# A two-block transformer kernel: one convolution tile instead of two on the vector engine, and the final sum by column halves

## The chip, the cores and the metric

The kernel runs on one core of one Trainium2 chip (trn2). The metric is the device time of one execution in microseconds (us). Engines: PE (TensorE, matrix products; PEld is its weight load), DVE (VectorE), ACT (ScalarE), POOL (GpSimd), SP (SyncE, which here only issues transfers).

## What is computed

Everything is float32, for 256 tokens of width 1024. A first block (two layers of mixer, feed-forward and gated side input) runs first and isn't touched. A second block follows, cut here to what matters:

```
h = rmsnorm(x, norm_mix_g) * (1 + sc1) + sh1
u = h @ w_in + b_in;  a, gt = split(u, 2);  u = a * sigmoid(gt)          # [256, 1024]
y = depthwise causal convolution of u, 31 taps per channel, + b_dw
y = silu(layernorm(y, ln_g, ln_b)) @ w_out
x = x + g1 * y
h = rmsnorm(x, norm_ffn_g) * (1 + sc2) + sh2
x = x + g2 * moe(h)      # 32 experts in 4 groups, top 2 in one group, hidden width 512
return rmsnorm(x, final_g)
```

## The kernel before, in words

**Order of work.** The program fixes the order on each engine by hand; every engine takes its instructions in program order. Three helpers place work between the matrix products of a stage: `fill` (lines 101 to 104) runs a function after so many products, `background` (lines 114 and 115) gives one small piece of work after every 12th or, from line 1418 on, every 10th product, and `prep` (lines 155 to 177) loads the next weight block (1 MB, SP) and splits an earlier one into a high and a low float32r part (ACT copies the high part, DVE subtracts; tiles `hl`). A float32 product is made of three products of such parts (`mm3`, `passes`).

**Convolution stage.** The 1024 channels are eight tiles of 128, with channels on partitions and 256 tokens along the row. For tiles 0 to 2 the input product is made token-major and turned (lines 1287 to 1306, `turn_u`); for tiles 3 to 7 it is made channel-major (`conv_in_proj`, step `i3` to `i7`, 48 products each). `conv_u` (line 1176) makes the gate with ACT and DVE. The tiles below `ONDVE` (line 1860: 2, so tiles 0 and 1) are convolved on DVE: `conv_dve` (line 1244) puts 31 taps per tile, each a `scalar_tensor_tensor` of 128x256, into `background`. The other tiles are convolved on PE: `u` goes to DRAM (`ud`, issued by POOL, line 1194) and comes back four-fold shifted (`u4`, four transfers issued by SP, line 1199; step `r`), POOL builds the diagonal tap blocks (`conv_taps_w`, line 1170; three buffers), and `conv_pe` (line 1257, steps `c2` to `c7`) makes 32 products, takes up to 8 pieces of background, and then lets ACT or DVE read the result into `yc`. The steps run in the order of `TG["plan"]` (line 1887): `R` and `t` prepare the router, `s` (`conv_pivot`, line 1271) computes the mean of two tiles (`PIVOT`, line 1889), which is subtracted from all, and `p` calls `prep`.

**Layer norm.** `conv_sums` (line 1210) squares each tile on ACT and adds tile and square into running sums: on DVE for tiles 0 and 1 and for the last two (`LATE`, tiles 6 and 7), on POOL for the others. After the last tile PE reduces the sums over the partitions (line 1458), DVE and POOL make mean and inverse deviation, PE spreads them (`mb`, `rb`), and per tile DVE subtracts and scales, ACT applies silu and makes the high part, DVE the low part (lines 1484 to 1494). `warm(n)` (line 123) issues n products whose result nobody reads. Then comes the product with `w_out`, the router and the experts.

**Experts.** Sixteen pairs of experts run one after the other; a pair takes twelve weight blocks of 1 MB in six steps of two (gate 0 and 1, up 2 and 3, down 4 and 5). `preload` (line 1120) issues block q into slot q % 21 as soon as the 21 slots allow; all are SP's. `down` (line 1636) turns the hidden values, multiplies by the two down blocks, and makes a high and a low part `yh`, `yl` that `combine2` of the next pair adds into the four PSUM banks `acc`. For the last pair `way_back` (line 1599) gives a plain float32 matrix, and `down` multiplies the result by a row of gains (`scaled`).

**The end.** Before the last pair's down product `gather_up` moves `acc` to SBUF and adds x; `acc` is zeroed by products with `zo` (line 1773). Then a loop of n_more rounds (line 1787; it runs for experts with more than 64 tokens) follows, and after it `finish`: eight float32 products into `acc` (`combine`, line 1671, four of 512 columns), DVE adds, ACT squares with a row sum, POOL the power, `spread(1)` (line 1713: the final gain row over all partitions, PE and then a copy), four DVE products, and four output transfers from SP.

Of the kernel before, what the change touches and what calls it, by code (L numbers as in the profile page):

```python
# [18 lines left out]
D = 1024  # L19
# [21 lines left out]
def kernel(ctx, tc, A, out, stop=None):  # L41
# [1119 lines left out]
    squares = cp.tile([128, 4, 256], F32, name="squares", tag="row")  # L1161
# [8 lines left out]
    def conv_taps_w(m):  # L1170

        taps[m] = cu.tile([128, 32, 32], F32, name="taps", tag="taps", bufs=3)
# [3 lines left out]
    def conv_u(m, pt):  # L1176
        sg = cu.tile([128, 256], F32, name="sg", tag="sg", bufs=2)
        act(sg, pt[:, 256:512], AF.Tanh, scale=0.5, bias=hbias[:, 8 + m:9 + m])
        a_ = cu.tile([128, 256], F32, name="a_", tag="a_", bufs=2)
        act(a_, pt[:, 0:256], AF.Identity, scale=0.5, bias=hbias[:, m:m + 1])  # L1180
# [6 lines left out]
        stt(u[:, 30:286], sg, 1.0, a_, ADD, MUL)  # L1187
# [8 lines left out]
        def back(q=SP):  # L1196
            u4[m] = cu.tile([128, 4, 284], F32, name="u4", tag="u4", bufs=3)
            for j in range(4):
                q.dma_start(u4[m][32 * j:32 * j + 32],
# [7 lines left out]
    sums = {"pool": None, "dve": None}  # L1207
    kept, squared = [], []

    def conv_sums(m):  # L1210

        sq = squares[:, len(squared) % 2, :]
# [3 lines left out]
        if m < ONDVE:  # L1216
            kept.append(new)
            if len(kept) == 2:
                sums["dve"] = small.tile([128, 2, 256], F32, name="sums", tag="xf")
                for i in range(2):  # L1220
                    tt(sums["dve"][:, i, :], kept[0][i], kept[1][i], ADD)
        elif m in LATE:
            for i in range(2):
                if m == LATE[0]:
                    tt(sums["dve"][:, i, :], sums["dve"][:, i, :], sums["pool"][:, i, :], ADD)
                tt(sums["dve"][:, i, :], sums["dve"][:, i, :], new[i], ADD)
        elif sums["pool"] is None:
            sums["pool"] = squares[:, 2:4, :]
            for i in range(2):
                G.tensor_copy(sums["pool"][:, i, :], new[i])  # L1230
        else:
            for i in range(2):
                tt(sums["pool"][:, i, :], sums["pool"][:, i, :], new[i], ADD, e=G)
# [49 lines left out]

    first_w = [nxt(True) for _ in range(3)]
    pm = [psum("mm") for _ in range(3)]
    um, us = {}, {}
    for h in range(2):
# [4 lines left out]
        for m in range(3):  # L1292
# [4 lines left out]
            um[m, h] = cu.tile([128, 256], F32, name="um", tag="um", bufs=4)  # L1297
# [121 lines left out]
    for m in range(ONDVE, ONDVE + 3):  # L1419
        conv_taps_w(m)  # L1420
    for step in TG["plan"].split():
# [3 lines left out]
        elif step in "ra":  # L1425
            while reads:
                reads.pop(0)(SP if step == "r" else S)
        elif step == "o":
            preload(len(moe_w) + 1)
        elif step[0] == "c":  # L1430
            conv_pe(m)
            if m < 5:
                conv_taps_w(m + 3)
# [17 lines left out]
    cs_ = [psum("aux"), psum("aux")]  # L1451
    mb, rb = psum("tp"), psum("tp")
# [3 lines left out]
    for i in range(2):  # L1456
        for h in range(2):
            T.matmul(cs_[i][:, h:h + 1], sums["dve"][:, i, h * 128:(h + 1) * 128], per_d, start=True, stop=True)
        if i == 0:
            V.tensor_copy(mo_[:, 0:2], cs_[0][:, 0:2])  # L1460
            tt(mo_[:, 2:4], mo_[:, 0:2], mo_[:, 0:2], MUL)
# [3 lines left out]
    stt(lv[:, 0:2], cs_[1][:, 0:2], EPS, mo_[:, 2:4], ADD, SUB)  # L1465
# [133 lines left out]
    def way_back(oh_g, n, exact=False, into=None):  # L1599
# [4 lines left out]
        if exact:  # L1604
# [5 lines left out]
        og_ = into or moe.tile([128, 2, 128], F32, name="ogT", tag="ogT", bufs=1)  # L1610
        V.tensor_copy(og_[:n], tp[:n, 0:256].rearrange("p (h t) -> p h t", h=2))  # L1611
        return og_
# [23 lines left out]
    def down(hid, weights, n_e, y, before=lambda j: None, scaled=False, gates_of=None):  # L1636
# [8 lines left out]
        py = [pbank("w"), pbank("w")]  # L1645
        for b in range(4, 6):
            ws = weights(b)
            before(b)
            for kk in range(2):
                k = 2 * (b - 4) + kk  # L1650
                for c in range(2):
                    for e in range(n_e):
                        T.matmul(py[c][64 * e:64 * e + 64, :], hT[:, k, 64 * e:64 * e + 64],  # L1653
                                 ws[e][:, kk * 1024 + c * 512:kk * 1024 + (c + 1) * 512],
                                 start=k == 0, stop=k == 3)
        if scaled:
            for c in range(2):
                sl = slice(512 * c, 512 * c + 512)
                tt(y[:n, sl], py[c][:n], end[0][:n, sl], MUL)
        else:  # L1660
            gc = gates_of()
            for c in range(2):
                sl = slice(512 * c, 512 * c + 512)
                act(yh[:, sl], py[c], AF.Copy, scale=gc)
                stt(yl[:, sl], py[c], gc, yh[:, sl].bitcast(F32), MUL, SUB)
# [40 lines left out]
    def start_ends():  # L1706
# [4 lines left out]
        end.extend([rows_[:, 0:D], rows_[:, D:2 * D], R, ring.tile([128, 2048], F32, name="raw", tag="raw")[:, 0:D]])  # L1711
# [39 lines left out]

    for i in range(NP):
        def weights(b, i=i):
# [3 lines left out]

        final = i == NP - 1

        def back(j, i=i, prev=prev, final=final):  # L1760
# [6 lines left out]
            if j == 1:  # L1767
                backs[i] = way_back(onehots[i], 128, not final)
            if i == NP - 2 and j == 5:
                start_ends()  # L1770
            if final and j == 5:
                for a in acc.values():
                    T.matmul(a, zo[:, 0:1].to_broadcast([1, 128]), zo[:, 1:2].to_broadcast([1, 512]), start=True, stop=False)
# [4 lines left out]
        hid = expert(weights, 2, (lambda: spread(0)) if final else None, None if i else start, 128 * (i % 2))  # L1778
        down(hid, weights, 2, end[3] if final else None, back, scaled=final, gates_of=lambda i=i: backs[i][1])
        prev = backs[i]  # L1780


    bt = rtile("bt", 1, pool=moe)
    V.memset(bt, 0.0)
    spare = nexts.tile([128, 2048], F32, name="nw", tag="nw")
    n_more = nc.values_load(nblk[0:1, 0:1], min_val=0, max_val=7)
    with tc.For_i(0, n_more, 1):
        oe = spare[:, D + 256:D + 288]
        ts(oe, upto, bt, None, ALU.is_gt)
        stt(oe, before, bt, oe, ALU.is_le, MUL)  # L1790
        tmp = moe.tile([128, 32], F32, name="more", tag="more")
        sel = moe.tile([128, 8], F32, name="sel")

        def pick(j, src):
            tt(tmp, src, oe, MUL)
            red(sel[:, j:j + 1], tmp, ADD)
        for h in range(2):
            pick(h, rank[:, h, :])
            pick(2 + h, gate[:, h, :])
        pick(4, before)  # L1800
        pick(5, iota64[:, 0:32])
        tt(sel[:, 6:7], bt, sel[:, 4:5], SUB)
        ts(sel[:, 6:7], sel[:, 6:7], 1.0, 64.0, ADD, MUL)
        ts(sel[0:1, 5:6], sel[0:1, 5:6], FAR, None, ADD)
        eid = moe.tile([1, 1], I32, name="eid")
        V.tensor_copy(eid, sel[0:1, 5:6])
        e_reg = nc.values_load(eid[0:1, 0:1], engines=(mybir.EngineType.SP,), min_val=0, max_val=NEXP - 1)
        oh_r = spare[:, D + 288:D + 544].rearrange("p (h t) -> p h t", h=2)
        oh_g = moe.tile([128, 2, 128], F32, name="oh", tag="oh_g", bufs=1)
        for h in range(2):  # L1810
            tt(sel[:, h:h + 1], sel[:, h:h + 1], sel[:, 6:7], SUB)
            for t_, sc in ((oh_r, rstd[h][:, 0:1]), (oh_g, sel[:, 2 + h:3 + h])):
                ts(t_[:, h, 0:64], iota64, sel[:, h:h + 1], sc, EQ, MUL)
        gather(oh_r, 64)
        og_ = way_back(oh_g, 64, into=spare[:, D:D + 256].rearrange("p (h t) -> p h t", h=2))

        def weights(b):
            t_ = wring.tile([128, 2048], F32, name="wr", tag="wr")
            SP.dma_start(t_, A["moe"][bass.ds(e_reg, 1), b].rearrange("a p n -> p (a n)"))
            return [t_]  # L1820
        hid = expert(weights, 1)
        y2 = spare[:, 0:D]
        down(hid, weights, 1, y2, scaled=True)
        for h in range(2):
            combine(h, og_, y2, False, False, 64)
        ts(bt, bt, 1.0, None, ADD)
    last = {}
    R, frow = end[2], end[1]

    def finish(h):  # L1830
        for c in range(2):
            sl = slice(512 * c, 512 * c + 512)
# [192 lines left out]
```

## Time and profile before

| what | us |
|---|---|
| median of three runs | 1257.26 (1253.07 to 1257.48) |
| the profiled execution, its own time | 1258.29 |
| its span in the profile | 1256.5 |
| PE, busy | 1191.1 (95%) |
| DVE, busy | 655.1 (52%) |
| ACT, busy | 481.4 (38%) |
| POOL, busy | 76.0 (6%) |

The profile counts microseconds from the start of the span. A row of the timeline gives start, duration, engine, line of the kernel, operation, output and inputs, and how many like instructions were merged; in square brackets stands how long the engine had been idle before and what ended that. The first block ends at about 659 us, the convolution stage runs to about 750, its output product and the router to about 796, the experts to about 1230, and the end to 1256.5. Durations of matrix products are pipelined, so two of them overlap in a row; one float32 product is two records.

### The profile page before, as it was taken

The numbers are of one execution on the slowest core, as the hardware profiler recorded it, in microseconds if no ns is written. First come the engines' busy times: TensorE is split into PE (matmuls) and PEld (weight loads), VectorE is DVE, ScalarE is ACT, GpSimd is POOL, SyncE is SP. The second block draws the span as 40 slices with busy tenths as digits, with TensorE's granted clock in tenths as the row PEclk, the third lists the DMA queues.
The fourth block names the chain that finished last, engine by engine and source line by source line (L and its number), as shares of the span: only waits on it lengthen the run. The fifth ranks groups of instructions, "written<-read, shape, count | busy, mean of one in ns | idle before, by whom it ended". The sixth has DMA issues, their size and how long they took to land. (4 is left out here: it accounts for less than half of the span.)

```text
span 1256.5 us, 15660 instructions
## 1 busy us (share of the span) xinstructions
PE 1191.1 (95%) x6064; PEld 816.7 (65%) x6067; DVE 655.1 (52%) x1112; ACT 481.4 (38%) x800; POOL 76.0 (6%) x105
## 2 busy tenths in 40 slices
PE   7999999999889999999998979999999999898996
PEld 5888888888777788888887947444444444343432
DVE  6767777677767687765464985422112221111114
ACT  7546544446775474444364523311101111010111
POOL 1101000001030000000003240000000000000000
PEclk9999999999999999999998989999999999999998
DMA  9644787774533189765543768699999999999992
GB/s 333 234 171 184 262 288 264 282 301 145 188 142 113 46 329 374 282 239 196 201 162 146 262 210 326 260 421 420 419 420 420 419 420 420 420 420 421 420 419 97
DMA packets 59947, 361.14 MB, mean 287 GB/s; under 512 B 7200, under 2 KB 10432, under 8 KB 21600
## 3 DMA queue, kind: packets, MB, share of 16 engines
q1 hardware_dynamic: 58752, 357.21, 73.2%
q0 software_dynamic: 976, 2.92, 0.7%
q8 instruction: 48, 0.79, 0.2%
q14 instruction: 27, 0.22, 0.1%
q10 hardware_dynamic: 144, 0.00, 0.0%
HBM read 358.15 MB, written 1.96 MB: 287 GB/s over the span
## 5 line engine op out<-in xcount | busy, mean ns | idle before, releaser
L111 PE MATMUL mm<-hl,xTh 128*128 128x512 f32 (+3 forms) x1376 | 422.1, 386 | 11.7 <-ACT hl L66 6.2
L70 DVE TENSOR_TENSOR hl<-raw,hl 128x1024 fp32r<-128x1024 f32 (+3 forms) x240 | 283.6, 1212 | 88.5 <-ACT hl L66 84.8
L111 PEld LDWEIGHTS mm<-hl,xTh 128*128 128x128 f32 x1376 | 257.0, 191 | 61.8 <-ACT hl L66 6.6
L66 ACT ACTIVATE hl<-raw 128x1024 fp32r<-128x1024 f32 (+3 forms) x240 | 240.7, 1033 | 137.3 <-PE mm L111 108.6
L111 PE MATMUL mm<-hl,xTl 128*128 128x512 f32 (+3 forms) x688 | 266.1, 387 | 2.5 <-DVE xTl L70 2.5
L111 PEld LDWEIGHTS mm<-hl,xTl 128*128 128x128 f32 x688 | 131.4, 191 | 26.0 <-DVE xTl L70 3.2
L70 DVE TENSOR_TENSOR hid<-gu,hid 128x512 f32<-128x512 f32 x16 | 11.1, 692 | 194.6 <-PE gu L1624 194.6
L111 PE MATMUL mm<-hl,aTh 128*128 128x512 f32 x352 | 109.0, 390 | 0.0
L1624 PE MATMUL gu<-hl,xg 128*64 128x512 f32 x392 | 100.9, 594 | 5.9 <-DMA hl<-in_moe_dram 5.9
L1624 PEld LDWEIGHTS gu<-hl,xg 128*64 128x64 f32 x392 | 35.0, 137 | 61.9 <-issue 50.2
L111 PEld LDWEIGHTS mm<-hl,aTh 128*128 128x128 f32 x352 | 66.1, 188 | 13.6
L79 DVE SCALAR_TENSOR_TENSOR yhl<-w,gc,yhl 128x512 fp32r<-128x512 f32 x30 | 22.4, 751 | 97.5 <-ACT yhl L66 95.7
L111 PE MATMUL mm<-hl,aTl 128*128 128x512 f32 x176 | 68.9, 391 | 0.0
L1624 PE MATMUL gu<-wr,xg 128*64 128x512 f32 x216 | 62.3, 595 | 5.8 <-DMA wr<-in_moe_dram 5.8
L80 DVE SCALAR_TENSOR_TENSOR ada<-ada,crow 128x1024 f32<-128x1024 f32 x48 | 58.4, 1220 | 8.0 <-DMA ada<-in_ada_dram 8.0
L66 ACT ACTIVATE yhl<-w,gc 128x512 fp32r<-128x512 f32 x30 | 20.5, 687 | 106.3 <-PE w L1653 106.3
L1653 PE MATMUL w<-hl,hid 128*64 128x512 f32 x184 | 48.9, 605 | 2.8 <-DVE ogT L1611 2.8
L66 ACT ACTIVATE xg<-w,modc,moe_g 128x256 f32<-128x256 f32 x32 | 18.1, 565 | 85.4 <-PE w L1594 85.4
L66 ACT ACTIVATE hid<-gu 128x512 f32<-128x512 f32 x16 | 9.6, 597 | 102.0 <-PE gu L1624 102.0
L1624 PE MATMUL gu<-raw,xg 128*64 128x512 f32 x152 | 44.7, 594 | 1.1 <-DMA raw<-in_moe_dram 1.1
L1624 PEld LDWEIGHTS gu<-wr,xg 128*64 128x64 f32 x216 | 20.4, 137 | 38.3 <-issue 25.9
L1624 PE MATMUL gu<-ew,xg 128*64 128x512 f32 x152 | 43.7, 594 | 0.4 <-DMA ew<-in_moe_dram 0.4
(459 smaller groups left out, 1503.9 us busy)
## 6 DMA issues: line engine op xcount, KB each, us to landing
raw<-in_dense_dram SPq DMA_DIRECT2D x108, 1024.0 KB, 5.2
hl<-in_moe_dram SPq DMA_DIRECT2D x72, 1024.0 KB, 19.8
wr<-in_moe_dram SPq DMA_DIRECT2D x45, 1024.0 KB, 19.9
ew<-in_moe_dram SPq DMA_DIRECT2D x29, 1024.0 KB, 19.9
raw<-in_moe_dram SPq DMA_DIRECT2D x27, 1024.0 KB, 19.9
ada<-in_ada_dram SPq DMA_DIRECT2D x48, 512.0 KB, 7.5
nw<-in_moe_dram SPq DMA_DIRECT2D x18, 1024.0 KB, 19.9
raw<-in_dense_dram SPq DMA_DIRECT2D x8, 512.0 KB, 7.1
```

The source lines that it names most:

```text
L66: return S.activation(o, i, f, bias=bias, scale=scale)
L70: return (e or V).tensor_tensor(o, a, b, op=op)
L79: return V.scalar_tensor_tensor(o, a, s, b, op0=op0, op1=op1)
L80: return V.scalar_tensor_tensor(o, a, s, b, op0=op0, op1=op1, accum_out=accum_out)
L111: T.matmul(o, lhsT, rhs, start=start, stop=stop_)
L1624: T.matmul(o[64 * e:64 * e + 64, :], xg[:, k, s0 + 64 * e:s0 + 64 * e + 64], ws[e][:, kk * 512:(kk + 1) * 512], start=k == 0, stop=k == 7)
L1653: T.matmul(py[c][64 * e:64 * e + 64, :], hT[:, k, 64 * e:64 * e + 64], ws[e][:, kk * 1024 + c * 512:kk * 1024 + (c + 1) * 512], start=k == ...
```

## The change

It does the following.

- `ONDVE` goes from 2 to 1: tile 1 is convolved on PE (a new step `c1`), with its own trip of `u` through DRAM. `PIVOT` is tiles 1 and 2.
- Tap blocks have four buffers (`TAPS`), and the first four are built on POOL ahead of the first input products; block m + 4 is built behind `conv_pe(m)`.
- The plan alternates input products and convolutions. Step `r` leaves the newest tile's reads for the next `r`; step `a` issues all, now on SP too.
- `conv_u` writes ACT's linear part into `u` itself. The turned products lie in `halves_u`.
- The running sums are all on POOL, up to tile 5. For tile 6 PE reduces the running sums and tile 6's own values into four PSUM banks, and tile 7's on top of them (`stat_sums`), instead of additions on DVE and one reduction at the end.
- `LN_AHEAD` 2 becomes 5, and `warm` in front of the output product 10 becomes 8.
- The down blocks' columns are stored in halves of 512; the last two blocks are loaded as four halves of 4 KiB per partition, all at the place of the last one.
- The last pair uses `yh` and `yl` for its first column half and a float32 product for the second; its gate and gain factors are applied in one DVE operation. `spread(1)` moves in front of the last pair's up product. The zeroing products go from four to two.
- At the end both row sums get one power; row half 1 is scaled on ACT and sent from ACT's queue, row half 0 on DVE and from SP.

```diff
 preload
-            pieces = 2 if q == 6 * NEXP - 1 else 1
-            for c in range(pieces):
-                sl = slice(2048 // pieces * c, 2048 // pieces * (c + 1))
-                SP.dma_start(t_[:, sl], A["moe"][2 * pair + r % 2, r // 2, :, sl])
+            if q < 6 * NEXP - 2:
+                SP.dma_start(t_, A["moe"][2 * pair + r % 2, r // 2])
             moe_w.append(t_)
+            if q == 6 * NEXP - 1:
+                for c in range(2):
+                    for e in range(2):
+                        sl = slice(1024 * c, 1024 * c + 1024)
+                        SP.dma_start(moe_w[q - 1 + e][:, sl], A["moe"][2 * pair + e, 5, :, sl])
...
 conv_u
-        a_ = cu.tile([128, 256], F32, name="a_", tag="a_", bufs=2)
-        act(a_, pt[:, 0:256], AF.Identity, scale=0.5, bias=hbias[:, m:m + 1])
...
-        stt(u[:, 30:286], sg, 1.0, a_, ADD, MUL)
+        act(u[:, 30:286], pt[:, 0:256], AF.Identity, scale=0.5, bias=hbias[:, m:m + 1])
+        stt(u[:, 30:286], sg, 1.0, u[:, 30:286], ADD, MUL)
...
+    def stat_sums(new, first, last):
+        for i in range(2):
+            for h in range(2):
+                if first:
+                    cs_[i, h] = psum(("tp", "aux")[i])
+                T.matmul(cs_[i, h][:, 0:1], new[i][:, h * 128:(h + 1) * 128], per_d, start=first, stop=last)
 conv_sums
-        elif m in LATE:
-            for i in range(2):
-                if m == LATE[0]:
-                    tt(sums["dve"][:, i, :], sums["dve"][:, i, :], sums["pool"][:, i, :], ADD)
-                tt(sums["dve"][:, i, :], sums["dve"][:, i, :], new[i], ADD)
+        if m in LATE:
+            if m == LATE[0]:
+                stat_sums(sums, True, False)
+            stat_sums(new, False, m == LATE[-1])
...
+    for m in range(ONDVE, ONDVE + TAPS):
+        conv_taps_w(m)
     first_w = [nxt(True) for _ in range(3)]
...
-    for m in range(ONDVE, ONDVE + 3):
-        conv_taps_w(m)
...
-            while reads:
-                reads.pop(0)(SP if step == "r" else S)
+            while len(reads) > (step == "r"):
+                reads.pop(0)()
...
 down
+            if final and b == 5:
+                for kk in range(2):
+                    for e in range(2):
+                        part(b, kk, 0, e)
+                out(0)
+                act(yh[:, 0:512], y[:, 0:512], AF.Copy)
+                tt(yl[:, 0:512], y[:, 0:512], yh[:, 0:512].bitcast(F32), SUB)
+                for h in range(2):
+                    T.matmul(acc[h, 1], zo[:, 0:1].to_broadcast([1, 128]), zo[:, 1:2].to_broadcast([1, 512]), start=True, stop=False)
+                for kk, e in ((0, 0), (1, 0), (0, 1), (1, 1)):
+                    part(b, kk, 1, e)
+                out(1)
+                return
...
+    def spread_ends():
+        spread(0)
+        spread(1, on_dve=(0, 1))
...
+    for h in range(2):
+        T.matmul(acc[h, 0], og_[:, h, :], yh[:, 0:512], start=True, stop=False)
+    more_blocks()
...
+    for h in range(2):
+        T.matmul(acc[h, 0], og_[:, h, :], yl[:, 0:512], start=False, stop=True)
+    for h in range(2):
+        combine(h, og32, y, False, True, cs=(1,))
+    for c in range(2):
+        sl = slice(512 * c, 512 * c + 512)
         for h in range(2):
             tt(R[:, h, sl], R[:, h, sl], acc[h, c], ADD)
+            act(sq, R[:, h, sl], AF.Square, scale=D ** -0.5, accum_out=ss[:, c, h:h + 1])
+    stt(ms[:, 0, :], ss[:, 0, :], EPS, ss[:, 1, :], ADD, ADD)
+    power(ms[:, 1, :], ms[:, 0, :], 2)
+    last = [ms[:, 1, h:h + 1] for h in range(2)]
+    for c in range(2):
+        sl = slice(512 * c, 512 * c + 512)
+        tt(fin[:, sl], R[:, 1, sl], frow[:, sl], MUL)
+    for c in range(2):
+        sl = slice(512 * c, 512 * c + 512)
+        stt(R[:, 0, sl], R[:, 0, sl], last[0], frow[:, sl], MUL, MUL)
+        SP.dma_start(out[0, 0:128, sl], R[:, 0, sl])
+        act(fin[:, sl], fin[:, sl], AF.Copy, scale=last[1])
+        S.dma_start(out[0, 128:256, sl], fin[:, sl])
...
-ONDVE = 2
-LN_AHEAD = 2
+ONDVE = 1
+LN_AHEAD = 5
+TAPS = 4
...
-    "w": (0, 0, 0, 3, 10, 0, 19, 4, 5, 2),
-    "plan": "R i3 i4 r i5 i6 t r c2 i7 c3 s c4 r p p p c5 c7 c6",
+    "w": (0, 0, 0, 3, 8, 0, 19, 4, 5, 2),
+    "plan": "i3 r i4 r c1 R i5 r c2 s i6 t r c3 i7 r c4 p p p c5 a c6 c7",
 }
-PIVOT = (2, 3)
+PIVOT = (1, 2)
```

## Rows read from the trace of the kernel before

**Rows 1.** The page's first line.

```profile
span 1256.5 us, 15660 instructions
```

**Rows 2.** Windows: window, its us; busy us (count) PE, PEld, DVE, ACT, POOL; PEclk, DMA share, GB/s.

```profile
820.00:840.00 20.00, 19.70 (x104) 9.01 (x101) 4.84 (x11) 3.28 (x6) 0.00 (x0) 1.00 1.01 422
...
1220.00:1240.00 20.00, 17.18 (x68) 5.88 (x66) 6.25 (x10) 0.60 (x1) 0.00 (x0) 0.91 0.50 206
```

**Rows 3.** Timeline of SP, the first expert slot filled again.

```profile
799.72 0.33 SPq L1138 DMA_DIRECT2D ew<-in_moe_dram  x1
```

**Rows 4.** Timeline of PE, convolution stage and start of its output product.

```profile
690.65 0.28 PE L111 MATMUL mm<-xTh,hl 128*128 128x256 f32 x1
...
714.36 3.66 PE L1261 MATMUL mm<-u,taps 128*32 128x256 f32 x64
...
728.78 7.11 PE L1261 MATMUL mm<-u,taps 128*32 128x256 f32 x128
740.44 9.57 PE L1261 MATMUL mm<-u,taps 128*32 128x256 f32 x128 [4.54 <-POOL taps L70]
752.25 1.88 PE L1458 MATMUL aux<-per_d,sums 128*128 128x1 f32 x8 [2.25 <-DVE sums L70]
...
756.16 3.79 PE L128 MATMUL aux<-ones_b 128*128 128x512 bf16 x10
759.60 0.81 PE L111 MATMUL mm<-hl,xTh 128*128 128x512 f32 x2
```

**Rows 5.** Timeline of DVE, the same stage.

```profile
725.47 3.25 DVE L79 SCALAR_TENSOR_TENSOR yc<-u,wtap,yc 128x256 f32<-128x256 f32 x8
...
750.93 0.48 DVE L79 SCALAR_TENSOR_TENSOR yc<-mm,vc,shift 128x256 f32<-128x256 f32 x1
...
756.41 2.08 DVE L70 TENSOR_TENSOR yc<-yc,tp 128x256 f32<-128x256 f32 x6 [0.95 <-PE tp L1469]
```

**Rows 6.** Windows of 2 us, columns as in rows 2.

```profile
742.00:744.00 2.00, 2.00 (x24) 0.93 (x20) 2.00 (x6) 0.00 (x0) 0.00 (x0) 0.50 0.81 184
...
756.00:758.00 2.00, 2.00 (x7) 0.83 (x6) 1.59 (x5) 1.10 (x3) 0.00 (x0) 0.50 0.99 418
```

**Rows 7.** Timelines of POOL and DVE at the first tap blocks.

```profile
672.06 6.29 POOL L70 TENSOR_TENSOR taps<-wcv,eye 128x1024 f32<-128x1024 f32 x3 [1.14 <-DMA wcv<-in_w_conv_dram]
...
676.62 2.28 DVE L70 TENSOR_TENSOR xTl<-xf,xTh 128x512 fp32r<-128x512 f32 x1
```

**Rows 8.** Timeline of SP; DMA issues of 696:699, 702:705, 717:720 (KB each, us to landing).

```profile
695.43 5.60 SPq L153 DMA_DIRECT2D raw<-in_dense_dram  x3
718.08 1.94 SPq L1199 DMA_DIRECT2D u<-ud  x4
...
raw<-in_dense_dram SPq DMA_DIRECT2D x1, 1024.0 KB, 6.7
...
u<-ud SPq DMA_DIRECT2D x2, 142.0 KB, 4.1
...
u<-ud SPq DMA_DIRECT2D x4, 142.0 KB, 5.3
```

**Rows 9.** Timelines of PE, ACT and DVE, last pair and end.

```profile
1212.00 3.65 PE L1624 MATMUL gu<-hl,xg 128*64 128x512 f32 x14 [1.33 <-DMA hl<-in_moe_dram]
1215.58 1.98 PE L1717 MATMUL w<-raw,ones 1*128 1x512 f32 x4
...
1232.18 0.64 PE L1653 MATMUL w<-hl,hid 128*64 128x512 f32 x1 [2.82 <-DVE ogT L1611]
...
1237.52 3.65 PE L1653 MATMUL w<-ew,hid 128*64 128x512 f32 x16
...
1243.34 5.40 PE L1671 MATMUL acc<-raw,ogT 128*128 128x512 f32 x8 [2.16 <-issue]
...
1249.56 0.63 ACT L67 ACTIVATE hid<-raw 128x512 f32<-128x512 f32 x1
...
1250.65 2.74 DVE L79 SCALAR_TENSOR_TENSOR raw<-raw,fr 128x512 f32<-128x512 f32 x4
```

More of the change, by code (lines that the diff above doesn't have):

```diff
@@ L1455 @@
     W_ = TG["w"]
[L1456 to L1461, printed above, removed]
+    for h in range(2):
+        V.tensor_copy(mo_[:, h:h + 1], cs_[0, h][:, 0:1])
+    tt(mo_[:, 2:4], mo_[:, 0:2], mo_[:, 0:2], MUL)
+    mb, rb = psum("tp"), psum("tp")
     warm(W_[2])
@@ L1597, in gather2, with way_back @@
                 gather_out(2 * g + i, tp[:, i, :], 256)
-    def way_back(oh_g, n, exact=False, into=None):
+    def way_back(oh_g, n, into=None):
         tp = pbank("w")
@@ L1634, in expert, with down @@
         return hid
-    def down(hid, weights, n_e, y, before=lambda j: None, scaled=False, gates_of=None):
+    def down(hid, weights, n_e, y, before=lambda j: None, gates_of=None, final=False):
         n = 64 * n_e
@@ L1645, in down, with part, out @@
         py = [pbank("w"), pbank("w")]
+        def part(b, kk, c, e):
+            k = 2 * (b - 4) + kk
+            T.matmul(py[c][64 * e:64 * e + 64, :], hT[:, k, 64 * e:64 * e + 64],
+                     ws[e][:, (2 * c + kk) * 512:(2 * c + kk + 1) * 512], start=k == 0, stop=k == 3)
+        def out(c):
+            sl = slice(512 * c, 512 * c + 512)
+            if gates_of is None:
+                tt(y[:n, sl], py[c][:n], end[0][:n, sl], MUL)
+                return
+            gc = gates_of()
+            if final:
+                stt(y[:, sl], py[c], gc, end[0][:, sl], MUL, MUL)
+            else:
+                act(yh[:, sl], py[c], AF.Copy, scale=gc)
+                stt(yl[:, sl], py[c], gc, yh[:, sl].bitcast(F32), MUL, SUB)
         for b in range(4, 6):
@@ L1648, in down @@
             before(b)
+            if final and b == 5:
[10 more added lines that the diff above has]
+                out(1)
+                return
             for kk in range(2):
-                k = 2 * (b - 4) + kk
                 for c in range(2):
                     for e in range(n_e):
[L1653 to L1665, printed above, removed]
+                        part(b, kk, c, e)
+        for c in range(2):
+            out(c)
     acc = {(h, c): pbank("acc") for h in range(2) for c in range(2)}
@@ L1767, in back @@
             if j == 1:
-                backs[i] = way_back(onehots[i], 128, not final)
+                backs[i] = way_back(onehots[i], 128)
             if i == NP - 2 and j == 5:
                 start_ends()
-            if final and j == 5:
-                for a in acc.values():
-                    T.matmul(a, zo[:, 0:1].to_broadcast([1, 128]), zo[:, 1:2].to_broadcast([1, 512]), start=True, stop=False)
         if i:
@@ L1777 @@
             ones2[0] = two_pairs(i + 1)
-        hid = expert(weights, 2, (lambda: spread(0)) if final else None, None if i else start, 128 * (i % 2))
-        down(hid, weights, 2, end[3] if final else None, back, scaled=final, gates_of=lambda i=i: backs[i][1])
+        hid = expert(weights, 2, spread_ends if final else None, None if i else start, 128 * (i % 2))
+        down(hid, weights, 2, end[3] if final else None, back, gates_of=lambda i=i: backs[i][1], final=final)
         prev = backs[i]
-    bt = rtile("bt", 1, pool=moe)
@@ L1784 @@
[L1784 to L1796, printed above, removed]
-        for h in range(2):
[L1798 to L1826, printed above, removed]
@@ L1847 @@
-    spread(1, on_dve=(0,))
-    for h in range(2):
-        finish(h)
+    R, frow = end[2], end[1]
+    og_, y = prev[0], end[3]
+    og32 = og_.bitcast(F32)
+    ss = stats.tile([128, 2, 2], F32, name="fs", bufs=1)
+    ms = stats.tile([128, 2, 2], F32, name="fr", bufs=1)
+    for h in range(2):
+        T.matmul(acc[h, 0], og_[:, h, :], yh[:, 0:512], start=True, stop=False)
+    more_blocks()
+    sq = moe.tile([128, 512], F32, name="hid", tag="hid", bufs=1)
+    fin = nexts.tile([128, 2048], F32, name="nw", tag="nw")[:, 0:D]
```

117 lines of the change are left out of this document (69 added, 48 removed).

## The prediction

> **What bounds the kernel now.** I read the page first, then windows for the stages, then the timelines of each engine over the two places that the change touches.
>
> The experts are bound by the weight transfers. From 820 us on the DMA engines are full at about 420 GB/s, and in the last such window they are busy half of it, so they stop near 1230 [rows 2]. A 1 MB block takes 1.05 MB / 420 GB/s = 2.5 us. Saturation starts when the first pair gives a slot back, at 799.7 [rows 3], and from there the bytes are fixed. So whatever the convolution stage wins or loses moves 799.7, and the end moves with it, one for one, as long as the 21 slots are filled by then.
>
> In the convolution stage PE runs without a gap from 690.65 to 728.78 + 7.11 = 735.89, then idles 4.54 us until POOL has built a tap block, and then takes 9.57 us for two tiles that took 7.11 before [rows 4]. PE's granted clock is at half (0.50 of 2.4 GHz) after that idle time, and again after the 2.25 us in front of the sums [rows 4, 6]. The last tap product ends at 740.44 + 9.57 = 750.0, DVE reads it only 0.9 us later, and the output product starts at 759.6 [rows 4, 5]. The end, from about 1230, is a chain in which PE, DVE and the loop take turns.
>
> **Part 1, to the last tap product.** Tile 1 leaves DVE: 31 taps of 3.25/8 = 0.41 us, 12.6 us of DVE time [rows 5]. With it goes the backlog that held up DVE's reads, and the POOL wait behind them. POOL builds the blocks a buffer ahead, so I cost the 4.54 us at zero; the cover is that block m + 4 has three steps to be built in, and if it's gone the wait is back. PE gains a tile: 3.66 us. It also gains the reductions at tile 6: four products over the running sums, during which DVE and ACT make tile 6's values, then four more, about the 1.88 us of four such products now [rows 4]. PE without a stall and at full clock is then
>
> 690.65 + 45.24 (the unbroken stretch) + 3.66 + 7.11 (the last two tiles at the full rate) + 1.9 = 748.5.
>
> The stall to price is `c1`. Four input products and a few small ones fill 690.65 to 714.36, so `i4` ends near 702.5. Tile 1's reads stand in SP's queue behind the dense load that now goes out as the second of three in 695.43 to 701 [rows 8], near 697.5. Four issues take 1.94 us, so the last is out at 699.4. Nothing before shows tile 1's reads; the nearest rows land in 4.1 and 5.3 us, the latter with two dense loads just ahead [rows 8]. So the data is there at 703.5 to 704.7, a stall of 1.0 to 2.2 us. I take 1.5: **750.0, no change** (from -1.5, no stall, to +2, a stall with a second of clock loss). The Trainium skill, "DMA: Bandwidth & Descriptors", section "Queues, rings and completion order", says that each DMA engine consumes the descriptors of one queue in ring order. By that rule the reads come behind the whole dense load, which is the slow rival below.
>
> Moved and hidden: one more `ud` write on POOL and four more reads on SP. Reads 1 and 2 pass in front of a dense load, whose split is only in `i6`, 10 us later; the last tile's reads pass in front of the first expert blocks, which have until 800. ACT now waits until a `u` buffer is free, which the write of two tiles earlier frees; zero, since an input product of 23.7/4 = 5.9 us lies between. A fourth tap block on POOL (6.29/3 = 2.1 us) lies beside the second half of the input split, where one DVE operation already takes 2.28 us [rows 7]; it can cost 0 to 0.5, and I take 0, since PE reaches those operands 2 us later.
>
> **Part 2, from there to the output product.** Now 759.60 - 750.01 = 9.6 us. The late DVE read (0.9, it becomes about 0.3) and the DVE additions in front of the sums (2.25 us of PE's wait, of which reading and squaring the last tile stay, 0.5 + 0.4 and hand-overs) go; two small DVE operations come (0.2 each). That is 1.4 less. `warm` loses two products of 3.79/10 = 0.38 us, 0.76 [rows 4]. Five subtractions in front of the scale instead of two (0.35 each) fit into the 0.95 us that DVE waits there, but for 0.1 [rows 5]. Together 2.1 at most, 2.5 if PE keeps its full clock. Against that: if the clock falls as now and comes back when it does now, the output product begins inside the slow stretch, 1.4 us of it, and loses 0.7; and it can't pass the first low part, which DVE makes behind six operations of 2.08 us [rows 5]. So 0.9 to 2.5; I take **-1.5**, nearer the low end because the 0.50 windows stand just there [rows 6].
>
> **Part 3, the experts.** The stored order of the down columns changes no product. The last but one block is issued one step later in the program, but it waits in a full queue anyway. Zero, covered by the saturated queue.
>
> **Part 4, the last pair and the end.** PE waits for weights at 1212.0 [rows 9], and two more blocks come 5 us later, at 1217.0. Today's spread of the gain row runs from 1215.6 to 1217.5, so it costs half a microsecond; a second one, 1.98 us, starts where the weights are already there and delays the up product by all of it. `way_back` for the last pair is then a sum and a mask instead of one copy, +0.4 before PE gets its bank back, in a wait that already shows as 2.82 us [rows 9]. So the first down block ends 2.35 us later than its 1236.2.
>
> From there to the end of the span it is 20.3 us now. After the change, step by step:
> - second down block, first column half 1.8 to 2.3; two zeroing products 0.5 to 0.7; second half 1.8, or 2.6 because its products no longer alternate between the two experts' columns (3.65 for both halves now) [rows 9];
> - two float32r products 0.5, loop entry 2.16, two more products 0.5;
> - two float32 products instead of four: half of 5.40, 2.7, or 1.8 at full clock (alone, one takes two of the 3.65/8 = 0.46 that side-by-side ones take) [rows 9];
> - last addition 0.25 + 0.69; square and row sum 0.9; statistic 0.3; power 0.7 to 1.5 with the row gain on DVE beside it;
> - two DVE products instead of four, 2.74/2 = 1.4 [rows 9], ACT doing the other row half; transfer and close 3.1 as now.
>
> Sum 16.4 to 19.6, middle 18.0: 2.3 less. With the 2.35 in front it is **0.0**, bounds -1.6 to +1.6: the spread only moves from the one place to the other.
>
> **The sum.** 0.0 - 1.5 + 0 + 0.0 = -1.5 us. Against the profiled execution's own 1258.29 (span 1256.5 [rows 1] and 1.8 around it) that is 1256.8. That execution lies 1.0 above the median of the runs shown, so against the median of 1257.26 I predict **1255.8**. All bounds together give -5.6 to +2.7, 1251.7 to 1260.0.
>
> **The rivals.**
> - *Full clock and a hidden spread (chance 0.20).* PE has no long gap left until 748.5, keeps 2.4 GHz through layer norm, and the up product of the last pair waits for weights longer than I read. For it: both slow windows follow gaps that the change shortens [rows 4, 6]. Against it: the sums still leave PE nearly idle, and 1217.0 comes out of two rows that agree. It gives -1.5 - 2.5 - 1.6 - 1.98 = -7.6, 1249.7.
> - *Tile 1 comes late, slower than before (0.17).* The reads start only when the dense load has landed, 697.5 + 6.7 = 704.2 [rows 8], and need another 1.9: `c1` starts at 706, a stall of 3.6. As after 2.25 and 4.54 us of idle time the clock falls to 1.2 GHz, and some 5 us at half rate cost 2.5. Part 1 becomes -1.5 + 3.6 + 2.5 = +4.6, the sum +3.1, 1260.4. It decides from about 2 us of stall on. For it: the 6.7 and 5.3 us. Against it: the first reads of now land in 4.1 us behind a dense load 4 us older. The ring-order rule named above would make it so; the trace leaves it open, as rows of both kinds exist.
> - *The win doesn't reach the end (0.05).* The slots aren't full when the experts start, so transfers begin no earlier. Against it: the DMA is idle before 799.7. It gives the end alone, 1257.
>
> **How the numbers follow.** My own case has 0.58. A measurement of this kernel can tell about 0.5%, 6.3 us, from no change: faster means under 1251.0, slower over 1263.5. Faster gets most of the first rival and the edge of my own case, 0.19; slower the far edge of the late tile, 0.09; the same 0.72. The range leaves out one in ten on each side: from the first rival's 1249.7 to the second's 1260.4, rounded to 1249.5 and 1260.5.
>
> **What would show it.** Right: no `taps` wait for PE; the last tap product near 750; the output product 7 to 8.7 us behind it; the first reload of an expert slot near 798; an up product of the last pair near 1217.5; a stretch of 18 us behind the first down block. Wrong: a PE gap of over 2 us in front of `c1` with a clock of 0.5 behind it, or one in front of the last tile, or experts that start at another time than the output product's shift says.

## The result, and the profile after

The changed kernel takes 1264.63 us (median of 5 runs, 1260.12 to 1265.58), beside 1255.76 for the kernel before on the same chip: a ratio of 1.0062 [1.0039, 1.0085]. It's slower, by 8.9 us between the medians; 1255.8 was forecast, with 1260.5 as the upper end. The profiled execution is the fastest of the five, 1260.12 us with a span of 1258.3.

First the timeline of PE, convolution stage, changed kernel (rows of [rows 4]). The first line is the stage's first product with weights; the product with the scaled diagonal `dg`, from which the expectations of e1 and e2 count, comes 3.1 to 3.2 us ahead of it (663.29 here, 659.47 before).

```profile
666.43 0.39 PE L111 MATMUL mm<-hl,xTh 128*128 128x256 f32 x1 [0.94 <-DVE xTh L283]
...
709.09 5.35 PE L1266 MATMUL mm<-u,taps 128*32 128x256 f32 x64 [3.91 <-DMA u<-ud]
...
740.34 10.57 PE L1266 MATMUL mm<-u,taps 128*32 128x256 f32 x192
...
752.71 3.66 PE L1266 MATMUL mm<-u,taps 128*32 128x256 f32 x64
...
759.45 1.90 PE L128 MATMUL aux<-ones_b 128*128 128x512 bf16 x8
761.69 0.74 PE L111 MATMUL mm<-hl,xTh 128*128 128x512 f32 x2 [0.35 <-ACT xTh L66]
```

The same first product in the kernel before:

```profile
662.68 0.39 PE L111 MATMUL mm<-hl,xTh 128*128 128x256 f32 x1 [0.93 <-DVE xTh L283]
```

So 3.75 us are lost in the first block, whose code is the same. One pair of executions wouldn't show that by itself: in the twelve profiled kernels that have the addresses of before (before, e1, e3 to e12), this product starts anywhere from 659.8 to 663.4. But 666.43 lies above all of them. Behind that, the wait for a tap block is gone (three tiles run unbroken in 10.57), and tile 1 waits 3.91 us for its reads and then runs at half rate (5.35 instead of 3.66). From the last tap product (752.71 + 3.66 = 756.37) to the output product it is 5.3 us instead of 9.6.

SP's timeline and DMA issues of 690 to 712, changed kernel (KB each, median us from issue to landing): the reads go out right behind a dense load and land 7.3 us later.

```profile
697.67 2.60 SPq L153 DMA_DIRECT2D raw<-in_dense_dram  x2
700.36 9.33 SPq L1202 DMA_DIRECT2D u<-ud  x8
...
u<-ud SPq DMA_DIRECT2D x12, 142.0 KB, 7.3
```

The last pair and the end on PE, changed kernel (rows of [rows 9]):

```profile
1214.00 3.65 PE L1625 MATMUL gu<-hl,xg 128*64 128x512 f32 x14 [1.34 <-DMA hl<-in_moe_dram]
1217.58 3.79 PE L1738 MATMUL w<-raw,ones 1*128 1x512 f32 x8
1221.30 8.78 PE L1625 MATMUL gu<-hl,xg 128*64 128x512 f32 x32
...
1237.06 0.61 PE L1650 MATMUL w<-hl,hid 128*64 128x512 f32 x1 [3.26 <-DVE ogT L74]
...
1246.78 0.73 PE L1861 MATMUL acc<-yhl,ogT 128*128 128x512 f32 x2 [2.14 <-issue]
1247.35 1.88 PE L1692 MATMUL acc<-raw,ogT 128*128 128x512 f32 x4
```

From the last wait for weights to the span's end it is 1258.3 - 1214.00 = 44.3 us; before, 1256.5 - 1212.00 = 44.5. That looks as forecast, but the two executions ran it at different clocks. Behind the wait for DVE the granted clock falls in the profile of before and stays whole in that of the changed kernel (windows of before, then of the changed kernel: window, its us; busy us of PE, PEld, DVE, ACT, POOL; PEclk, DMA share, GB/s):

```profile
1230.00:1235.00 5.00, 2.82 (x10) 0.91 (x12) 2.09 (x4) 0.00 (x0) 0.00 (x0) 0.86 0.11 46
1235.00:1240.00 5.00, 5.00 (x20) 1.29 (x18) 0.00 (x0) 0.00 (x0) 0.00 (x0) 0.80 0.00 0
...
1235.00:1240.00 5.00, 2.94 (x14) 1.26 (x16) 1.88 (x4) 0.00 (x0) 0.00 (x0) 1.00 0.00 0
```

One profile (e2, the kernel before with an operand moved, below) shows the old end with the clock whole up to its last products, and there it takes 1257.1 - 1215.93 = 41.2 us:

```profile
1215.93 3.65 PE L1623 MATMUL gu<-hl,xg 128*64 128x512 f32 x14 [1.35 <-DMA hl<-in_moe_dram]
...
1236.11 0.64 PE L1652 MATMUL w<-hl,hid 128*64 128x512 f32 x1 [2.81 <-DVE ogT L1610]
...
1245.62 3.70 PE L1670 MATMUL acc<-raw,ogT 128*128 128x512 f32 x8 [2.16 <-issue]
```

The new end under the same condition takes 42.6 us (e1). So even there it is 1.4 us longer, and the agreement of 44.3 with 44.5 is luck.

### The profile page after: what moved, and what is told of

The parts are those of the page before. It is cut to its first block, busy times and chain, and to the rows that moved or that the text cites. A ratio compares the mean times of both kernels' runs of the same rounds, so it can differ in the third digit from the quotient of the medians.

```text
span 1258.3 us, 15805 instructions
## 1 busy us (share of the span) xinstructions
PE 1191.8 (95%) x6143; PEld 817.2 (65%) x6143; DVE 647.2 (51%) x1079; ACT 482.9 (38%) x802; POOL 76.3 (6%) x109
## 5 line engine op out<-in xcount | busy, mean ns | idle before, releaser
L1625 PE MATMUL gu<-raw,xg 128*64 128x512 f32 x152 | 44.5, 593 | 0.9 <-DMA raw<-in_moe_dram 0.9
```

The source lines that it names most:

```text
L1625: T.matmul(o[64 * e:64 * e + 64, :], xg[:, k, s0 + 64 * e:s0 + 64 * e + 64], ws[e][:, kk * 512:(kk + 1) * 512], start=k == 0, stop=k == 7)
```

## The experiments

The runs are called e1 to e15. e1 to e12 are 6 to 12 executions each, and their ratios are to executions of the kernel before on the same chip; the last three are one execution each. The chips differ between groups of runs, but the median of the kernel before lies between 1255.07 and 1255.67 us on all of them.

**1. The addresses.** The change stores the row sums of the end in two tiles instead of four, 64 bytes in all. The input tiles of the first block, allocated behind them, lie 64 bytes lower; the split weights `hl` stay where they were, since their pool is filled from the other side (`side="right"`). The run e1 gives the 64 bytes back:

```diff
     stats = ctx.enter_context(tc.tile_pool(name="stats", bufs=2))
+    shift_by(stats, 32)
```

Expected of e1:

> The changed kernel with 64 bytes of unused space put back beside its small statistics tiles, so that every tile of the first block lies at the address it had before. Theory A (addresses): the first block's products run 1% slower in the changed kernel because its operands moved by 64 bytes. Then the convolution stage's first product with the scaled diagonal comes at 659.5 us again instead of 663.3, and the whole is 3.5 to 4.5 us faster than the changed kernel: 1260 to 1261, ratio to before 1.003 to 1.004. Rival B (another cause, such as the order of the code or another chip): that product stays near 663 and the time near 1264.6.

1259.68 us (1255.62 to 1263.9, 12 runs), ratio 1.0036 [1.0020, 1.0052]; the stage's first product is at 663.03. And the other way round, the kernel before with its input operand 64 bytes lower:

```diff
-    shift_by(xp, 64)
```

Expected of e2:

> The kernel before with nothing changed but the 64 bytes between the residual tile and the split inputs left out, so that the split inputs, the weight ring and all tiles behind them lie 64 bytes lower, where the changed kernel has them. Theory A (addresses): 3.5 to 4.5 us slower than before, ratio 1.0028 to 1.0036, with the convolution stage starting near 663.3. Rival B: no change, ratio within 0.999 to 1.001.

1258.87 us, ratio 1.0034 [1.0018, 1.0051], first product at 666.99. The stage's first product of e1 and then of e2:

```profile
663.03 0.38 PE L112 MATMUL mm<-hl,xTh 128*128 128x256 f32 x1 [0.93 <-DVE xTh L284]
...
666.99 0.39 PE L111 MATMUL mm<-hl,xTh 128*128 128x256 f32 x1 [0.93 <-DVE xTh L282]
```

So 3.3 to 4.3 us of the loss are made by the place of the first block's operands, and appear and go with it. (3.3 is the difference of two ratios whose intervals overlap, so e2 and the starts of the stage carry this more than e1's time.) The pace of the block shows it too. SP waits there for DVE's split of the weights, so the distance between its loads follows that pace: kernel before and then e2 (183.61 - 160.96 = 22.65 us, 184.71 - 161.84 = 22.87); the changed kernel has 22.87 and e1 22.66.

```profile
160.96 0.33 SPq L153 DMA_DIRECT2D raw<-in_dense_dram  x1
...
183.61 0.33 SPq L153 DMA_DIRECT2D raw<-in_dense_dram  x1
```

```profile
161.84 0.33 SPq L153 DMA_DIRECT2D raw<-in_dense_dram  x1
...
184.71 0.33 SPq L153 DMA_DIRECT2D raw<-in_dense_dram  x1
```

**2. Tile 1's reads.** On top of the first run, tile 1's four reads go out one step sooner, ahead of the dense loads of the input product of tile 3:

```diff
-    "plan": "i3 r i4 r c1 R i5 ..."
+    "plan": "a i3 r i4 r c1 R i5 ..."
```

Expected of e3:

> As the first kernel, and tile 1's four reads are issued one step sooner, ahead of the dense loads of the input product of tile 3. Theory C (the reads wait in the queue's ring behind the 1 MB dense load, and the idle PE then loses its clock): PE's gap in front of tile 1's taps falls from 3.9 us to under 0.5, its 64 tap records take 3.7 us instead of 5.4, and the time falls by another 5 to 8 us to 1253 to 1256. Rival D (the DMA engines are simply full there and the load comes late instead): the gap stays over 2 us or moves to a later step, and less than 2 us is won.

1261.06 us, ratio 1.0044 [1.0026, 1.0062], no better than e1: the rival's case. DMA issues of 689 to 700 and PE of this kernel:

```profile
u<-ud SPq DMA_DIRECT2D x4, 142.0 KB, 2.9
...
699.92 3.66 PE L1267 MATMUL mm<-u,taps 128*32 128x256 f32 x64
...
740.25 6.49 PE L1267 MATMUL mm<-u,taps 128*32 128x256 f32 x64 [3.36 <-DMA u<-ud]
749.06 5.35 PE L1267 MATMUL mm<-u,taps 128*32 128x256 f32 x64 [0.45 <-DMA u<-ud]
```

Reads issued ahead of the loads landed in 2.9 us and tile 1 doesn't wait. But PE is then early for the last tiles, whose `u` isn't back: the gap comes later. Then the reads on another queue:

```diff
+            q_ = S if m == 1 else SP
             for j in range(4):
-                SP.dma_start(u4[m][32 * j:32 * j + 32],
+                q_.dma_start(u4[m][32 * j:32 * j + 32],
```

Expected of e4:

> As the first kernel, and tile 1's four reads are issued by ACT instead of SP, at the same place in the program. They stand on another ring than the dense load. Theory C: the reads land in 3 to 5 us instead of 7.3, PE's gap falls to under 2 us. Rival D (engines full): they land in about 7 us as before, and the gap stays near 3.9. ACT gives up about 2 us for the issues, so the time may not gain: 1256 to 1261.

1263.69 us, ratio 1.0056 [1.0034, 1.0078]. The four reads in ACT's queue, 690 to 712, and PE:

```profile
raw<-in_dense_dram SPq DMA_DIRECT2D x4, 1024.0 KB, 8.7
...
u<-ud ACTq DMA_DIRECT2D x4, 142.0 KB, 8.1
...
704.96 5.35 PE L1268 MATMUL mm<-u,taps 128*32 128x256 f32 x64 [3.79 <-DMA u<-ud]
```

They land no sooner, and `c1` waits 3.79 us. A queue of their own didn't help them against two loads under way; of the two edits only issuing them earlier did.

**3. Each half alone.** First the convolution stage's hunks with the old end, then the end's hunks with the old stage (and the 64 bytes). Their edits are the diff shown above, cut at the experts.

Expected of e5:

> The convolution stage's part of the change alone, with the old end, down columns and zeroing, and so the old addresses. Theory (what is left of the loss behind the addresses lies in the end): the stage gains 1.5 to 2 us in spite of the stall at tile 1, as the profile of the changed kernel shows it, and the end is the old one: 1253.5 to 1255 beside 1255.7. Rival (the stall and the clock behind it cost more in most executions than in the profiled one): 1257 or more.

1256.03 us, ratio 1.0008 [0.9995, 1.0020]: between theory and rival, no change.

Expected of e6:

> The end's part of the change alone, with the old convolution stage, and 64 unused bytes so that the addresses are the old ones. Theory: the new end costs 4 to 6 us in most executions, since PE's clock falls behind its wait for DVE in the last pair and stays low for longer: 1259.5 to 1261.5, with a wide spread between runs. Rival (the end is worth nothing either way, as forecast; the loss is made by the convolution stage): 1255 to 1256.5.

1258.76 us (1254.78 to 1261.42), ratio 1.0022 [1.0008, 1.0037], 0.7 below the theory's range and 2.3 above the rival's. With the 0.34% of the addresses (0.26% by e1) the parts add up to 0.64% (0.56%); 0.62% was measured. The end's profile shows where it loses (PE's timeline, then windows with the columns as above):

```profile
1232.68 1.08 PE L1652 MATMUL w<-hl,hid 128*64 128x512 f32 x1 [3.25 <-DVE ogT L75]
1237.01 2.95 PE L1652 MATMUL w<-ew,hid 128*64 128x512 f32 x9
...
1245.18 1.22 PE L1863 MATMUL acc<-yhl,ogT 128*128 128x512 f32 x2 [2.15 <-issue]
1246.20 3.04 PE L1694 MATMUL acc<-raw,ogT 128*128 128x512 f32 x4
...
1230.00:1235.00 5.00, 2.32 (x6) 0.86 (x8) 2.50 (x5) 0.00 (x0) 0.00 (x0) 0.65 0.00 0
1235.00:1240.00 5.00, 5.00 (x17) 1.50 (x14) 0.00 (x1) 0.00 (x0) 0.00 (x0) 0.67 0.00 0
```

Behind the 3.25 us of waiting for DVE the clock falls: the granted clock is 0.50, 1.2 GHz, in every window of 2 us from 1232 to 1238. The first down product takes 1.08 instead of 0.61, nine of them 2.95 instead of 2.31 (that row in e7), the last four float32 ones 3.04 instead of 1.88. From the last wait for weights, at 1209.62, to the span's end at 1258.0 it is 48.4 us, 4 more than in the profile of the changed kernel. e3 and e4 fell the same way (48.4 and 50.4 us). Whether the clock falls differs from one execution to the next: in the profile of e1 it doesn't. Its 12 runs reach from 1255.6 us at a mean granted clock of 0.992 to 1263.9 at 0.984; the six with a mean of 0.989 or more have a median of 1257.3, the other six of 1262.2.

**4. The wait for DVE.** DVE stands in front of the last `way_back` with eight additions that nothing needs until `acc` is zeroed. They go behind it, in the changed kernel (old addresses) and in the kernel before:

```diff
-                if final:
-                    gather_up(j)
...
             if j == 1:
                 backs[i] = way_back(onehots[i], 128)
+                if final:
+                    gather_up(0)
+                    gather_up(1)
```

Expected of e7:

> The changed kernel with the old addresses, and the eight DVE operations that gather the sum and add x now stand behind the sum and the mask of the last way back, so that PE need not wait 3.3 us for DVE in front of the first down block. Theory (that wait brings the clock down): no wait there, full clock to the loop, 1252 to 1255 beside 1259.7 with the wait. Rival (the clock falls for another reason, such as the wait for weights earlier, or the wait for DVE is only followed by one for weights): 1258.5 to 1260.

1254.29 us (1251.95 to 1256.46), ratio 0.9991 [0.9978, 1.0004], 5.4 us under e1. PE has no gap there and the clock is whole:

```profile
1234.24 2.31 PE L1651 MATMUL w<-ew,hid 128*64 128x512 f32 x9
...
1241.77 0.73 PE L1863 MATMUL acc<-yhl,ogT 128*128 128x512 f32 x2 [2.15 <-issue]
1242.35 1.88 PE L1693 MATMUL acc<-raw,ogT 128*128 128x512 f32 x4
...
1230.00:1235.00 5.00, 5.00 (x24) 2.13 (x24) 3.79 (x7) 0.59 (x1) 0.00 (x0) 1.00 0.00 1
1235.00:1240.00 5.00, 4.63 (x20) 1.26 (x16) 4.15 (x8) 0.63 (x1) 0.00 (x0) 1.00 0.01 2
```

None of its 12 runs has a mean clock under 0.988; of e1's 12, five have. With the wait gone the falls behind it are gone, and wait and clock together are worth more than the 3.3 us of the gap: against e1's six runs at the higher clock e7 wins 3.0 us, about the gap alone, and against all twelve 5.4. The mean clock of a run also counts falls elsewhere (e10 below has no such wait, and 0.985 or 0.986 in five of its 12 runs), so it marks this fall only between kernels that are alike in the rest.

Expected of e8:

> The kernel before with the same one reordering and nothing else: the eight operations behind the copy of the last way back. Theory: the 2.8 us of PE's wait go, and the half clock behind them too: 1251.5 to 1253. Rival (weights come next, or the loop entry sets the time): 1255 to 1256.

1253.09 us, ratio 0.9986 [0.9973, 0.9998]: 2.3 us between the medians, just short of the theory. PE now waits 0.90 us for the additions in front of the zeroing, which the expectation had not counted:

```profile
1229.85 0.37 PE L1774 MATMUL acc<-zo 1*128 1x512 bf16 x1 [0.90 <-DVE raw L70]
```

**5. The rest of the end.** In e7, the final gain row is spread behind the last products again:

```diff
 def spread_ends():
     spread(0)
-    spread(1, on_dve=(0, 1))
...
+    spread(1, on_dve=(0, 1))
     stt(ms[:, 0, :], ss[:, 0, :], EPS, ss[:, 1, :], ADD, ADD)
```

Expected of e9:

> The last kernel of the changed end (additions behind the way back) with the final gain row spread where it was, behind the last products, instead of in front of the last pair's up product. Theory (ahead of the up product it costs its 1.9 us, and the up product behind it 8.8 to 10.0 us instead of 8.15, since PE's clock falls behind the eight one-row products; behind the last products its copies fit in the 1.1 us that DVE waits for ACT's squares): 1251 to 1252.5 beside 1254.3. Rival (the up product waits for weights anyway, or the copies at the end cost as much): 1254 to 1255.5.

1254.00 us, ratio 0.9989 [0.9978, 0.9999]: the rival, no gain. The profile does show the parts, spread 1.98 instead of 4.18 and up product 8.17 instead of 10.04, and an end of 39.3 us instead of 42.6; but the profiled execution is one of the two fastest of the kernel, 2 us under its median. The places differ by less than these runs tell apart.

Expected of e10:

> The same mended end with the convolution stage of before and the old addresses. Theory (the stage as changed is worth nothing either way, its stall at tile 1 takes what the tap wait gave): within 1 us of the run with the changed stage, 1251 to 1252.5, and 1 to 2 under the kernel before with the additions later (1253.1), since halves, two products fewer and the shared power shorten the last stretch. Rival (the stage costs 0.6 as run alone, or gains 1.7 as the profile of the changed kernel read): 0.6 lower or 1.7 higher than that run.

1254.07 us, ratio 0.9990 [0.9977, 1.0002]: as e9, so the stage is worth nothing here either; and 1.0 above e8 instead of 1 to 2 below. Halves, a shared power and the float32r half show no gain.

**6. The order of the stage.** In e9, with PE given 6 us of other work before it needs tile 1, and tile 7's `u` made earlier:

```diff
-    "plan": "i3 r i4 r c1 R i5 r c2 s i6 t r c3 i7 r c4 p p p c5 a c6 c7"
+    "plan": "i3 r i4 r R i5 c1 r c2 s i6 t r i7 c3 r c4 p p p c5 a c6 c7"
```

Expected of e11:

> The mended end with the changed convolution stage in another order: the fifth input product in front of tile 1's taps and the seventh in front of tile 3's, so that the late reads have 6 us more to land and the last tile's u is made earlier. Theory (the stall at tile 1, 3.8 us and up to 1.7 of half clock behind it, is all that stands against the stage): 3.5 to 5 under the run in the old order, 1247 to 1249. Rival (the last two tiles' trips through DRAM are next in line, as when tile 1's reads went ahead): a gap of 2 to 4 us moves to the last tap products and the time stays within 1.5 us.

1250.00 us (1246.1 to 1252.82, 7 runs), ratio 0.9957 [0.9941, 0.9972]. That is 4.0 under e9, the theory's difference (the time comes out higher than expected because e9's did). In the profiles the stage is 2.5 us shorter, 93.2 from its first product to the output product instead of 95.7 in e9; where the rest of the 4.0 was won isn't shown. Of PE's gaps in the taps 1.24 us are left:

```profile
709.21 7.11 PE L1267 MATMUL mm<-u,taps 128*32 128x256 f32 x128
729.26 10.57 PE L1267 MATMUL mm<-u,taps 128*32 128x256 f32 x192
741.07 3.66 PE L1267 MATMUL mm<-u,taps 128*32 128x256 f32 x64 [1.24 <-POOL taps L71]
```

The same stage with the old end, its additions moved as in e8:

Expected of e12:

> The convolution stage in the new order with the end of before, of which only the additions are moved behind the way back. Theory (the stage is what gains, 4 us; of the end the one reordering is worth 2.3 and the rest of the new end nothing): 1248.5 to 1250.5, as the run with the whole mended end (1250.0). Rival (halves, the shared power and the float32r first half do shorten the end by 1 us or more): 1251 to 1252.5.

1252.32 us, ratio 0.9977 [0.9961, 0.9992], the rival's value. Here the mended new end is 2.3 us better, with the old stage it was 1.0 worse; what it is worth stays open within about 2 us. The same numbers leave the price of the order open: with the new end it wins 4.0 us (e9 to e11, whose intervals don't overlap), with the old end, against the old stage, 0.8 (e8 to e12, whose intervals do), where the profiles show the stage 1.7 us shorter (94.1 and 95.8). The fastest version is e11, faster than both kernels.

**7. What of the address counts.** The kernel before with the input operand, and all that is allocated behind it, 32 bytes lower, 32 higher and 64 higher (`shift_by(xp, 32)`, `96`, `128` instead of `64`):

Expected of e13:

> The kernel before with the split input and what follows it 32 bytes lower (distance to the weight tiles 96 or 32 modulo 128). Theory (what counts is that input and weights lie alike modulo 128 bytes, as before): the first product of the convolution stage at 666 to 667 instead of 660 to 663.4. Rival (only the one place 64 bytes lower is bad, or 32-byte steps that share a 64-byte line are): 660 to 663.4.

Expected of e14:

> The same 32 bytes higher. Theory (alike modulo 128): 666 to 667. Rival (higher is as good as the place of before): 660 to 663.4.

Expected of e15:

> The same 64 bytes higher, so at the same place modulo 128 as 64 bytes lower. Theory (alike modulo 128): 666 to 667, as there. Rival (a distance of more than 128 bytes counts, or the low place is bad by itself): 660 to 663.4.

The stage's first product comes at 673.84, 673.71 and 674.67, the times are 1267.56, 1263.61 and 1270.38 us. All three are worse than the place 64 bytes lower (666.99), so the rule of 128 bytes falls: 64 higher and 64 lower would be the same by it. The rivals miss as well, none stays at 660 to 663.4. The place of before is the best of five, but which operand against which, and by what rule, isn't settled, since the tiles behind it moved with it.

## Why the prediction was wrong, step by step

- **The first block** had no term in the sum: its code isn't touched, so I began to count at 690.65. The kernel before has four `shift_by` lines (196, 234, 589, 699) that put 32 or 64 unused bytes between tiles of this block; I passed over what they might be for. The block lost 3.75 us, through the allocation of a tile at the other end of the program. The runs of the first pair show this as 0.26 to 0.34% of the time.
- **Part 1** was forecast at 0 and is +2.6, counted from the stage's first product: 756.37 - 666.43 = 89.9 against 750.01 - 662.68 = 87.3 [rows 4]. The step that failed is the price of `c1`: 1.5, bounds 1.0 to 2.2, for a stall of 3.91 with 1.69 of half clock behind it. The late rival had 3.6 and 2.5. It took its price from the row of a dense load (6.7) [rows 8]; I took 4.1 and 5.3, and the reads took 7.3. The Trainium skill, "DMA: Bandwidth & Descriptors", section "Queues, rings and completion order", has each DMA engine consume a queue's descriptors in ring order. The 7.3 us behind a load and the 2.9 ahead of it agree, but they don't show that the order is the cause: in e4 the reads had a queue without a load ahead of them and took 8.1. The same section has an engine take turns between queues, packet by packet. By that I'd have expected a queue of their own to bring the reads sooner, and e4 doesn't show it. What held them up, the ring or DMA engines that were full, stays open. That tap blocks no longer hold up PE was right.
- **ACT's wait for a `u` buffer**, costed at zero, shows as 2.28 us in the profile; PE was waiting for `c1` beside it, and no run prices it alone.
- **Part 2** was forecast at -1.5 and is -4.3 (5.3 against 9.6), beyond the bound of -2.5: the clock stayed whole, which I had put into a rival, and `warm` took 1.90 instead of 3.79 [rows 4]. So parts 1 and 2 add up to -1.7 in the profiled pair, near the -1.5, by luck, through two wrong terms. From first product to output product, five profiled executions with the old stage (before, e2, e6, e8, e10) take 95.3 to 97.1 us and five with the new (after, e1, e5, e7, e9) 95.3 to 96.5: on the mean of these ten part 1 is +3.8 and part 2 -4.1, and there is no gain to speak of, as e5 says in time.
- **Part 3** was right: the first reload is 2.6 us later (802.36), the last wait for weights 2.0 later.
- **Part 4** was forecast at 0.0 with bounds of 1.6 either way; e6 measures 0.22%, +2.8. Two steps failed. The first is `way_back`'s 0.4 us "in a wait that already shows as 2.82". Their size was right (3.26), but that wait is the one behind which the clock falls, and I gave the clock no bound there, although the mean of 0.91 up to 1240 stands in [rows 2]. The fix, eight DVE operations moved, takes 5.4 us off. The second is the 2.3 us by which the rest was to be shorter. The 20.3 us that I took them from belong to an execution whose clock falls in them (5.40 for the float32 products [rows 9], 3.70 in e2). From the first down product behind the wait to the span's end it is 24.3 us before, 21.2 in the changed kernel, and 21.0 in e2, where the old end keeps its clock: the 3.1 us that the profiled pair shows are the clock's, and nothing is left of the 2.3. That rests on one profile of the old end; e9 to e12 leave the worth of the halves and the shared power open. The second spread lets the up product start 1.8 us later, near the 1.98 of the sum. What the product's end loses goes by the clock, for which the sum had no term here either: 0.7 us in e1, where it stays whole (the product takes 7.09 instead of 8.14), 2.5 in the changed kernel's profile (8.78) and 4.1 in e7's (10.04).
- **Chances.** Slower by over 0.5% had 0.09. Three steps failed together. One, `c1`, was in a rival, and by e5 it took no more than the rest of the stage gave; one was a wait without its clock, and one was in no part of the list. The last two make the loss.

## What to carry to other kernels

Before costing a change, see what it allocates: where a PE-bound stage runs on operands behind the resized tile, compare their addresses, and the rate of the untouched stage in both profiles. Price a wait of PE with the half-rate rows behind it, not by its own length, and ask first whether the work that causes it is needed that early. Before taking a gain out of a profile, see whether the row it is taken from ran at full clock. When a stall goes, see which transfer was hidden by it: reading tile 1 earlier only moved the gap, and the order that gave PE other work at that place won 4.0 us with one end and 0.8 with the other. That order also made tile 7's `u` earlier; reading tile 1 earlier with that as well wasn't run.

## What the runs showed of the hardware that was not expected

Moving an operand, and the tiles behind it, by 32 or 64 bytes in the partition changes the pace of products that run back to back, at a granted clock of 1.00. PE at the end of the first block, kernel before and then e13: three products (two on `xTh`, one on `xTl`) come every 0.68 and every 0.70 us; by the end of the block e13 is 11 us later.

```profile
656.25 0.61 PE L111 MATMUL mm<-hl,xTh 128*128 128x512 f32 x2
656.71 0.39 PE L111 MATMUL mm<-hl,xTl 128*128 128x512 f32 x1
656.93 0.61 PE L111 MATMUL mm<-hl,xTh 128*128 128x512 f32 x2
```

```profile
656.27 0.63 PE L111 MATMUL mm<-hl,xTh 128*128 128x512 f32 x2
656.74 0.39 PE L111 MATMUL mm<-hl,xTl 128*128 128x512 f32 x1
656.97 0.63 PE L111 MATMUL mm<-hl,xTh 128*128 128x512 f32 x2
```

And the executions of one kernel lie up to 9 us apart (e3's from 1257.5 to 1266.5), where a wait stands behind which the clock falls in some of them and not in others. Not all of such a spread is that wait's: e12 hasn't got it, and its runs go from 1248.0 to 1255.6.
